# Folding the query squares of the grouped-query heads to 64 rows, and taking their roots in two parts

## The chip, the cores and the metric

The kernel runs on one core of a Trainium2 chip. The metric is the device time of one execution in microseconds (us); the time before is the median of three runs, 1474.04 us (1473.47 to 1475.6). The profile is one execution recorded by the hardware, with five compute queues: PE (TensorE matmuls; PEld is its weight loads), DVE (VectorE), ACT (ScalarE), POOL (GpSimd) and SP (which issues transfers). 0.2% of the time is 2.95 us.

## The reference, cut to what matters

One step of a two-layer backbone over 512 latent tokens and 128 prompt tokens (640 columns in all). The second layer's mixer is grouped-query attention: 8 query heads of width 128, 2 key/value heads. Queries and keys are normalised per token and head, then rotated, then used in a softmax:

```python
def rms_norm(x, g):
    y = xf * lax.rsqrt(jnp.mean(xf * xf, axis=-1, keepdims=True) + RMS_EPS)
    return (y * g.astype(jnp.float32)).astype(x.dtype)
...
    q = rms_norm(q.reshape(b, L, GQA_HEADS, GQA_HEAD_DIM), q_norm)
    q = apply_rope(q, cos, sin)
    o = attend_blocked(q, jnp.concatenate([k, c_k], axis=1), jnp.concatenate([v, c_v], axis=1), GQA_SCALE)
```

What the change touches is the reciprocal root of the mean square of each token's query, for one head: 640 numbers per head. The rotation does not alter the sum of squares, and the root is one factor per token, so the kernel applies it late, as a scale inside the softmax's exponential.

## The kernel before, in words

Activations lie with features on the 128 partitions and tokens on the columns. Every large product is made of three matmuls of split operands (a high and a low part, so that precision is near fp32): `mm3` at line 183 and `proj` at line 188.

The part that matters is the loop over the 8 heads at line 1906. In head h's turn the PE queue interleaves four kinds of work, each cut into pieces:

- `s0` to `s4`: scores of head h for token tiles 0 to 4 (tile 4 is the prompt), into a two-bank PSUM tile `gs` of which there are two. After a piece come a maximum (DVE, line 1858), a bias `gb` = maximum times root (DVE, line 1868), the exponential with the root as scale (ACT, line 1869), a reciprocal (DVE) and a scaling (POOL, line 393). For tile 0 the part from the bias on is a piece of its own, `x0`.
- `q0` to `q7`: the projection of head h+1's queries, `q0` to `q3` for columns 0 to 319 and `q4` to `q7` for columns 320 to 639. At the end of each half `done` (line 1827) copies the sum out of PSUM (`gqc`, ACT), squares it (`gsq`, ACT, line 1830), rotates it (`gqr`, four DVE operations), and splits the result into `gqh` (ACT) and `gql` (DVE), the score weights of the next turn.
- `t0` to `t4`, `v0` to `v4`, `pt` and `pv`: transposes and value products of head h-1. A transpose piece puts four 128x128 blocks into a PSUM bank `gt`, which `pt_split` (line 395) empties by an ACT copy (`gts_..h`) and a DVE subtraction (`gts_..l`). `pt` does the same for the prompt (`gtp`). All `v` pieces sum into one bank, `go`.
- `r`: the root of head h. Five matmuls have the squares of one token tile as weights and two columns of ones as the moving operand; each is recorded as two passes. Then ACT takes the logarithm and an exponential (lines 1841 and 1842).

The order of these pieces on PE is written out by hand in `GQA_ORDER` (line 1905), and `run` (line 115) ties each piece behind the matmul before it. The other engines' orders are made by a planner, which takes what is ready in the plan's own time, earlier program lines first. Buffers are given out by that planner too: a tile takes a buffer of its tag once all readers of the earlier tile there are done.

PSUM has eight banks. Four belong to the two `gs` tiles. The other four have the tag "m" (line 91) and serve every other PSUM tile of this loop: `gq` (one half of a projection), `gt`, `gtp`, `go`, `gop` and `gr` (the roots).

The weights of the next projection are also split within the turn: an ACT copy (line 173) and a DVE subtraction `wgq` (line 174) of 128x1024.

The planner's order and the buffers follow from these lines:

```python
            return psp.tile([P, 512], F32, tag="m", bufs=4, name=name)
...
        return tp.tile([P, T], F32, tag="t", bufs=3, name=name)
```

Of the kernel before, what the change touches and what calls it, by code (L numbers as in the profile page):

```python
# [11 lines left out]
F32 = mybir.dt.float32  # L12
F32R = mybir.dt.float32r
AF = mybir.ActivationFunctionType
ALU = mybir.AluOpType
# [3 lines left out]
P = 128  # L19
# [32 lines left out]
def body(ctx, tc, xT, vecs, crow, wm0, wm0g1, wm0g, wm1, wA, wNV, wNA, wMK, wMV, wOA, wGQ, wGK, wGV, wOC,  # L52
# [3 lines left out]
    V, S, G = nc.vector, nc.scalar, nc.gpsimd  # L56
# [32 lines left out]
    def bank(name, kind="m"):  # L89
        if kind == "m":  # L90
            return psp.tile([P, 512], F32, tag="m", bufs=4, name=name)
        return ypool["pool"].tile([P, 512], F32, tag=kind, bufs=ypool["tags"][kind], name=name)
# [10 lines left out]
    def tmp(name):  # L103
        return tp.tile([P, T], F32, tag="t", bufs=3, name=name)

    def f(ap):
        return ap.bitcast(F32)
# [7 lines left out]
    def run(pieces):  # L115

        for piece in pieces:
            with tc.issue_after(PE.last.ins):
                piece()
# [7 lines left out]
    def named(prefix, pieces):  # L127
        return {f"{prefix}{i}": piece for i, piece in enumerate(pieces)}
# [6 lines left out]
    ones = main.tile([P, P], F32, name="ones")  # L135
    V.memset(ones, 1.0)
    eps = main.tile([P, 1], F32, name="eps")
    V.memset(eps, EPS)
    lnsc = main.tile([P, 1], F32, name="lnsc")
# [9 lines left out]
    def vcol(i):  # L149
        return vec[:, i:i + 1]  # L150
# [17 lines left out]
    def unit(src, n, name, lo="v", pool=None, bufs=3):  # L168

        raw = load(src, n, name + "r")  # L170
        t = (pool or wp).tile([P, 2, 1024], F32R, tag="w", bufs=bufs, name=name)
        hi, lw = t[:, 0, :n], t[:, 1, :n]
        S.activation(hi, raw, AF.Copy)
        (V if lo == "v" else G).tensor_tensor(lw, raw, f(hi), ALU.subtract)
        return hi, lw

    def after(inst, fn):
        if inst is None:
            return fn()
        with tc.issue_after(inst.ins):  # L180
            return fn()
# [13 lines left out]
    class Norm:  # L195
# [19 lines left out]
        def rstd(self, i):  # L215
            c0, c1 = HALF[i]
            pss = bank(f"{self.name}p{i}")
            PE.matmul(pss[:, :HT], ones, self.acc[:, c0:c1], start=True, stop=i not in self.alone)
            if i in self.alone:
                PE.matmul(pss[:, :HT], ones, self.alone[i], start=False, stop=True)  # L220
            S.activation(self.rs[:, c0:c1], pss[:, :HT], AF.Ln, bias=eps, scale=1.0 / self.n)
            S.activation(self.rs[:, c0:c1], self.rs[:, c0:c1], AF.Exp, scale=-0.5)
            return self.rs
# [273 lines left out]
    def lazy(fn):  # L497
        box = []

        def get():  # L500
            if not box:
                box.append(fn())
            return box[0]
        return get
# [128 lines left out]
    for kk in range(4):  # L633
# [3 lines left out]
        for j in range(2):  # L637
            k = 2 * kk + j
            a, b = wh[:, 512 * j:512 * (j + 1)], wl[:, 512 * j:512 * (j + 1)]
            for i in range(5):  # L640
                c0, c1 = P * i, P * i + P
# [264 lines left out]
    for h in range(8):  # L906
        p, r = divmod(h, 2)
# [8 lines left out]
        qh, ql, ks = [t[r] for t in nqk[p]]  # L916
        pieces = named("s", sc)
# [60 lines left out]
    def mla_scores(h, pts, beside):  # L978
        r = h % 2
        ll = tiny.tile([P, 4], F32, tag="ll", bufs=4, name=f"ml{h}")  # L980

        def piece(j):
            qh, ql = mqs[h]
            pss = bank2(f"ms{h}_{j}")
            kh, kl = [t[0] for t in k_tiles(r, h // 2)]
            scores(pss, (qh[:, P * j:P * j + P], ql[:, P * j:P * j + P]), kh, kl)
            if j in beside:
                beside[j](pss[:, :, HT:HT + P])
            nm = tiny.tile([P, 1], F32, tag="nm", name=f"mn{h}_{j}")
            V.tensor_reduce(nm, pss[:, :, :HT], AX.XY, ALU.max, negate=True)  # L990
            pt = cp.tile([P, T], F32, tag="mp", bufs=8, name=f"mp{h}_{j}")
            exps[h, j] = S.activation(halves(pt), pss[:, :, :HT], AF.Exp, bias=nm, accum_out=ll[:, j:j + 1])
            softmax_tail(pt, ll[:, j:j + 1], f"mr{h}_{j}", T)
            pts.append(pt)
        return [lambda j=j: piece(j) for j in range(4)]
# [40 lines left out]
    for h in range(8):  # L1036
        p, r = divmod(h, 2)
# [5 lines left out]
        qh, ql = mqs[h]  # L1043
        beside = {1: tail.pop("pt"), 3: tail.pop("pv")} if h and r == 0 else {}
        pieces = named("s", mla_scores(h, pts, beside))
# [676 lines left out]
    gp = sb.enter_context(tc.tile_pool(name="gp", bufs=1, reuse_waits="tile"))  # L1722
# [91 lines left out]
    nc.gpsimd.dma_start(o_gv, gvf[:, :256])  # L1814

    gqs, gexp = {}, {}

    def gqa_q(h):
        get = lazy(lambda: after(gqs[h - 1][3][0] if h > 1 else None, lambda: unit(wGQ[h], 1024, f"wgq{h}", lo="v" if h == 1 else "v")))
        qh = gp.tile([P, T], F32R, tag="gqh", bufs=2, name=f"gqh{h}")  # L1820
        ql = gp.tile([P, T], F32R, tag="gql", bufs=2, name=f"gql{h}")
        rq = tiny.tile([P, 5], F32, tag="rq", bufs=2, name=f"rq{h}")
        sq = tmp(f"gsq{h}")
        gqs[h] = qh, ql, rq, []
        out = []
        for c, (c0, c1) in enumerate(HALF):
            def done(ps, c=c, c0=c0, c1=c1):
                qc = tp.tile([P, HT], F32, tag="u", bufs=7, name=f"gqc{h}{c}")
                gqs[h][3].append(S.activation(qc, ps[:, :HT], AF.Copy))
                S.activation(sq[:, c0:c1], qc, AF.Square)  # L1830
                qr = tp.tile([P, HT], F32, tag="u", bufs=7, name=f"gqr{h}{c}")
                rope(qr, qc, vcol(V_GQ), c, f"gqr{h}{c}")
                S.activation(qh[:, c0:c1], qr, AF.Copy)
                V.tensor_tensor(ql[:, c0:c1], qr, f(qh[:, c0:c1]), ALU.subtract)
            out += pieces_of(f"gq{h}{c}", qbank, get, hh, hl, list(range(KT)), c0, c1, done)

        def rstd():
            pr = bank(f"gr{h}")
            for j in range(5):
                PE.matmul(pr[:, 2 * j:2 * j + 2], sq[:, P * j:P * j + P], ones[:, 0:2], start=True, stop=True)  # L1840
            S.activation(rq, pr[:, 0:10].rearrange("p (a b) -> p a b", b=2)[:, :, 0], AF.Ln, bias=eps, scale=1.0 / P)
            S.activation(rq, rq, AF.Exp, bias=lnsc, scale=-0.5)
        return out + [rstd]

    def gqa_scores(h, pts):
        v = h // 4
        ll = tiny.tile([P, 5], F32, tag="lg", bufs=4, name=f"gl{h}")

        def piece(j):
            qh, ql, rq, _ = gqs[h]  # L1850
            q = qh[:, P * j:P * j + P], ql[:, P * j:P * j + P]
            nm = tiny.tile([P, 1], F32, tag="nm", name=f"gn{h}_{j}")
            nb = tiny.tile([P, 1], F32, tag="nb", name=f"gb{h}_{j}")
            pss = bank2(f"gs{h}_{j}")
            if j < 4:
                pt = gp.tile([P, T], F32, tag="gp", bufs=8, name=f"gp{h}_{j}")
                scores(pss, q, kTh[v], kTl[v])
                V.tensor_reduce(nm, pss[:, :, :HT], AX.XY, ALU.max, negate=True)
                src, dst, n = pss[:, :, :HT], halves(pt), T
            else:  # L1860
                pt = gp.tile([P, P], F32, tag="gpp", bufs=1, name=f"gp{h}_{j}")
                src = pss[:, 0, :P]
                mm3(src, *q, kTh[v][:, 640:768], kTl[v][:, 640:768], True, True)
                V.tensor_reduce(nm, src, AX.X, ALU.max, negate=True)
                dst, n = pt, P

            def weigh():
                V.tensor_tensor(nb, nm, rq[:, j:j + 1], ALU.mult)  # L1868
                gexp[h, j] = S.activation(dst, src, AF.Exp, bias=nb, scale=rq[:, j:j + 1], accum_out=ll[:, j:j + 1])  # L1869
                softmax_tail(pt, ll[:, j:j + 1], f"gr{h}_{j}", n)  # L1870
                pts.append(pt)
            return weigh

        box = []
        rest = {f"s{j}": (lambda j=j: piece(j)()) for j in range(1, 5)}
        return {"s0": lambda: box.append(piece(0)), "x0": lambda: box[0](), **rest}
# [22 lines left out]
        return {"pt": prompt_t, "pv": prompt, **t}  # L1899

    open_y(s=2)
    *qp, rstd = gqa_q(0)
    run(qp)
    tail, oG = {}, []
    GQA_ORDER = "s0 r x0 t0 q0 s1 t1 q1 t2 s2 q2 v0 t3 s3 q3 v1 t4 s4 pt q4 v2 q5 q6 v3 q7 v4 pv"
    for h in range(8):
        oG.append(gp.tile([P, T], F32, tag="go", bufs=8, name=f"oG{h}"))
        pts = []
        pieces = gqa_scores(h, pts)
        pieces["r"] = rstd  # L1910
        if h < 7:
            *qp, rstd = gqa_q(h + 1)
            pieces.update(named("q", qp))
        sequence(GQA_ORDER, {**pieces, **tail})
        tail = gqa_values(h, pts, oG[h])
# [181 lines left out]
```

## Time and profile before

| | us |
|---|---|
| median of three runs | 1474.04 |
| profiled execution | 1473.37 |
| its span | 1471.5 |
| one head's turn with all four kinds of work | 18.07 |
| PE busy in the span | 1439.2 (98%) |

The span runs from the first to the last recorded instruction; 1.87 us of the execution's own time lie around it. In a timeline a row gives start, duration, engine, line, operation, tiles written and read, and in brackets the idle time ahead of it with what ended it. Matmuls overlap, so that on PE the distance between two starts is the price of an instruction, and the duration is not.

### The profile page before, as it was taken

To read this page: it belongs to the slowest core of one execution; us is meant where nothing else is said; L and a number is where in the kernel's file an instruction comes from. 1 tells how busy PE (TensorE), PEld (TensorE's weight loads), DVE (VectorE), ACT (ScalarE), POOL (GpSimd) and SP (SyncE) were. 2 spreads that over 40 slices of the span, in tenths; PEclk is the share of its full clock that TensorE was granted. 3 is DMA by queue.
4 is the path that set the end of the run, shared out by engine and by line. 5 is a ranking of instruction groups with operands and counts; after the bars stand their busy time and mean duration, and the time that the engine had idled before them with its cause. 6 is when DMAs were issued, how large, how long until landed. Compare 5 with 4: busy or idle time off the path is not lost.

```text
span 1471.5 us, 25831 instructions
## 1 busy us (share of the span) xinstructions
PE 1439.2 (98%) x9764; PEld 1388.8 (94%) x9764; DVE 1235.1 (84%) x2391; ACT 783.9 (53%) x1539; POOL 173.9 (12%) x270
## 2 busy tenths in 40 slices
PE   5999999999999999999999999999999999999997
PEld 3989978889999999999999999989999999999997
DVE  5877798877998888965997888888899898989976
ACT  5446687763755555531223656672656555555443
POOL 0046645420000000000000122220000000000000
PEclk9999999999999999999999999999999999999999
DMA  9653431025165555569764310115245555548572
GB/s 372 212 161 125 145 115 44 15 89 184 48 213 165 169 168 170 181 233 321 235 223 150 97 33 30 45 44 185 87 167 187 179 177 182 177 143 296 184 270 72
DMA packets 79636, 231.48 MB, mean 157 GB/s; under 512 B 8856, under 2 KB 13240, under 8 KB 79128
## 3 DMA queue, kind: packets, MB, share of 16 engines
q1 hardware_dynamic: 77152, 225.43, 45.7%
q10 hardware_dynamic: 1944, 3.48, 0.7%
q8 instruction: 76, 1.25, 0.3%
q0 software_dynamic: 416, 0.93, 0.2%
q14 instruction: 48, 0.39, 0.1%
HBM read 193.15 MB, written 36.66 MB: 156 GB/s over the span
## 4 chain that ended last, share of the span: by engine, by line
PE 86%; DVE 6%; ACT 4%; issue 2%; DMA 2%; POOL 1%; DVEq 0%; ACTq 0%; POOLq 0%
PE fg L64 21%; PE fd L64 9%; PE fgo L64 5%; PE fo L64 5%; PE fu L64 4%; PE gq L64 3%; PE fdo L64 2%; PE gs L64 2%; PE go L64 2%; PE fuo L64 1%; PE nq L64 1%; PE gt L68 1%; PE nk L64 1%; PE gvp L64 1%; PE mod L64 1%
## 5 line engine op out<-in xcount | busy, mean ns | idle before, releaser
L1664 DVE SCALAR_TENSOR_TENSOR junk<-wm,cb 128x1024 bf16<-128x1024 f32 x88 | 107.2, 1218 | 6.4 <-DMA wm<-in_wm 5.5
L64 PE MATMUL gq<-h10h,wgq 128*128 128x320 f32 x256 | 65.8, 316 | 0.0
L267 POOL TENSOR_SCALAR h10h<-h10t,gs,mods 128x320 fp32r<-128x320 f32 x4 | 3.9, 990 | 429.4 <-DVE h10t L261 427.1
L1404 ACT ACTIVATE wY<-s 128x1024 fp32r<-128x1024 f32 x38 | 40.3, 1061 | 25.4 <-PE fg L64 21.4
L1932 POOL TENSOR_TENSOR xr<-xw,fn1rs 128x320 f32<-128x320 f32 x2 | 1.7, 862 | 412.8 <-ACT fn1rs L235 412.8
L1404 ACT ACTIVATE wZ<-s 128x1024 fp32r<-128x1024 f32 x38 | 40.1, 1056 | 16.0 <-PE fd L64 11.7
L1405 DVE TENSOR_TENSOR wZ<-s,wZ 128x1024 fp32r<-128x1024 f32 x38 | 46.3, 1219 | 1.6
L1405 DVE TENSOR_TENSOR wY<-s,wY 128x1024 fp32r<-128x1024 f32 x38 | 46.3, 1219 | 0.3
L64 PEld LDWEIGHTS gq<-h10h,wgq 128*128 128x128 f32 x256 | 44.9, 189 | 0.6
L1513 DVE TENSOR_TENSOR sg<-up,sg 128x640 f32<-128x640 f32 x38 | 31.2, 822 | 15.8 <-ACT sg L1512 15.0
L1512 ACT ACTIVATE sg<-fg 128x320 f32<-128x320 f32 x38 | 16.7, 438 | 48.4 <-PE fg L64 48.4
L1534 ACT ACTIVATE p<-fd 128x320 f32<-128x320 f32 x38 | 16.6, 438 | 44.1 <-PE fd L64 44.1
L64 PE MATMUL gq<-h10l,wgq 128*128 128x320 f32 x128 | 39.4, 308 | 0.0
L1869 ACT ACTIVATE gp<-gs,gb,rq 128x640 f32<-128x640 f32 (+1 forms) x40 | 31.8, 796 | 13.2 <-DVE gb L1868 11.8
L64 PE MATMUL fg<-h01E,wW 128*128 128x320 f32 x228 | 36.6, 309 | 0.5 <-DVE g L1544 0.5
L64 PE MATMUL fg<-h11N,wZ 128*128 128x320 f32 x228 | 36.7, 309 | 0.0
L64 PE MATMUL fg<-h01q,wX 128*128 128x320 f32 x228 | 36.7, 309 | 0.0
L64 PE MATMUL fu<-h11q,wX 128*128 128x320 f32 x228 | 36.6, 309 | 0.0
L64 PE MATMUL fd<-h11q,wZ 128*128 128x320 f32 x228 | 36.6, 309 | 0.0
L64 PE MATMUL fd<-h01q,wZ 128*128 128x320 f32 x228 | 36.5, 309 | 0.0
L64 PE MATMUL fg<-h01C,wY 128*128 128x320 f32 x228 | 36.5, 309 | 0.0
L64 PE MATMUL fg<-h11q,wX 128*128 128x320 f32 x228 | 36.5, 309 | 0.0
(3421 smaller groups left out, 5299.4 us busy)
## 6 DMA issues: line engine op xcount, KB each, us to landing
wm<-in_wm SPq DMA_DIRECT2D x48, 512.0 KB, 4.2
mraw<-in_wm SPq DMA_DIRECT2D x8, 1024.0 KB, 13.1
mraw<-in_wm SPq DMA_DIRECT2D x14, 512.0 KB, 4.1
wmv<-in_wm0g SPq DMA_DIRECT2D x8, 512.0 KB, 4.1
wm<-in_wm0g SPq DMA_DIRECT2D x8, 512.0 KB, 5.1
ruo<-in_wFO SPq DMA_DIRECT2D x8, 512.0 KB, 3.9
rgo<-in_wFO SPq DMA_DIRECT2D x8, 512.0 KB, 5.3
x<-in_xT SPq DMA_DIRECT2D x8, 320.0 KB, 5.4
```

The source lines that it names most:

```text
L64: cls.last = nc.tensor.matmul(*a, **k)
L68: cls.last = nc.tensor.transpose(*a, **k)
L267: G.tensor_scalar(h[:, c0:c1], t, self.gsl[:, k, 0:1], self.ml[:, self.sh + k, 0:1], ALU.mult, ALU.add)
L1404: S.activation(h, src, AF.Copy)
L1405: V.tensor_tensor(w_, src, f(h), ALU.subtract)
L1512: last = S.activation(sg[:, 0:HT], g[:, :HT], AF.Silu, scale=-1.0)
L1513: V.tensor_tensor(sg, up, sg, ALU.mult)
L1534: S.activation(p5, b5[:, :HT], AF.Copy)
L1664: V.scalar_tensor_tensor(junk, raw, 1.0, cb[:, c, :], ALU.mult, ALU.mult, accum_out=mods[l][:, j0 + i, c:c + 1])
L1869: gexp[h, j] = S.activation(dst, src, AF.Exp, bias=nb, scale=rq[:, j:j + 1], accum_out=ll[:, j:j + 1])
L1932: G.tensor_tensor(x[k][:, c0:c1], root[1][k], nrm.rs[:, c0:c1], ALU.mult)
```

## The change

The squares of a half are written in two pieces of 64 rows (features 0 to 63 and 64 to 127), both on partitions 0 to 63. A new tile `fold` receives their sums, so that 64 rows hold what 128 held: rows 0 to 63 of a column block carry one token tile and rows 64 to 127 the next. Block 0 holds tiles 0 and 1, block 1 tiles 2 and 3, and block 2 tile 4 on its first 64 rows. A constant `two` of two columns, with ones on the upper or the lower 64 rows, then gives both tiles' sums in one product. So there are three products per head in place of five.

The roots are taken in two parts: block 0 (`n`, or `early` for head 0) in the turn before, between `q6` and `v3`; blocks 1 and 2 (`r`) in the head's own turn, now between `s1` and `t1`. Each part has its own PSUM bank and its own logarithm and exponential. The bias `gb` moves from DVE to ACT, and `x0` directly follows `s0`. The `t` tag has three buffers as before, and each head now takes two of them. For the second half the folding stands ahead of the low part's subtraction.

```diff
+    two = gp.tile([P, 2], F32, name="two")
+    V.memset(two, 0.0)
+    for r in range(2):
+        V.memset(two[64 * r:64 * r + 64, r:r + 1], 1.0)
...
-        sq = tmp(f"gsq{h}")
+        sq = [tmp(f"gsq{h}{r}")[0:64] for r in range(2)]
+        fold = gp.tile([P, 3, P], F32, tag="gfold", bufs=2, name=f"gfold{h}")
+        a, b = [t.rearrange("p (j n) -> p j n", n=P) for t in sq]
...
+        def folded(i, r, j, n):
+            V.tensor_tensor(fold[64 * r:64 * r + 64, i:i + n, :], a[:, j:j + 2 * n - 1:2, :], b[:, j:j + 2 * n - 1:2, :], ALU.add)
...
-                S.activation(sq[:, c0:c1], qc, AF.Square)
+                for r in range(2):
+                    S.activation(sq[r][:, c0:c1], qc[64 * r:64 * r + 64], AF.Square)
...
-                V.tensor_tensor(ql[:, c0:c1], qr, f(qh[:, c0:c1]), ALU.subtract)
+                if c == 0:
+                    V.tensor_tensor(ql[:, c0:c1], qr, f(qh[:, c0:c1]), ALU.subtract)
+                    folded(0, 0, 0, 1)
+                    folded(0, 1, 1, 1)
+                else:
+                    folded(1, 0, 2, 2)
+                    folded(1, 1, 3, 1)
+                    V.tensor_tensor(ql[:, c0:c1], qr, f(qh[:, c0:c1]), ALU.subtract)
...
-        def rstd():
-            pr = bank(f"gr{h}")
-            for j in range(5):
-                PE.matmul(pr[:, 2 * j:2 * j + 2], sq[:, P * j:P * j + P], ones[:, 0:2], start=True, stop=True)
-            S.activation(rq, pr[:, 0:10].rearrange("p (a b) -> p a b", b=2)[:, :, 0], AF.Ln, bias=eps, scale=1.0 / P)
-            S.activation(rq, rq, AF.Exp, bias=lnsc, scale=-0.5)
-        return out + [rstd]
+        def rstd(at):
+            pr = bank(f"gr{h}{at}")
+            for i in ((0,), (1, 2))[at]:
+                rows = slice(0, P if i < 2 else 64)
+                PE.matmul(pr[:, 2 * (i - at):2 * (i - at) + 2], fold[rows, i, :], two[rows], start=True, stop=True)
+            t = rq[:, (0, 2)[at]:(2, 5)[at]]
+            S.activation(t, pr[:, 0:2 + at], AF.Ln, bias=eps, scale=1.0 / P)
+            S.activation(t, t, AF.Exp, bias=lnsc, scale=-0.5)
+        return out + [lambda: rstd(0), lambda: rstd(1)]
...
-                V.tensor_tensor(nb, nm, rq[:, j:j + 1], ALU.mult)
+                S.activation(nb, nm, AF.Copy, scale=rq[:, j:j + 1])
...
-    *qp, rstd = gqa_q(0)
-    run(qp)
+    *qp, early, rstd = gqa_q(0)
+    run(qp + [early])
...
-    GQA_ORDER = "s0 r x0 t0 q0 s1 t1 q1 t2 s2 q2 v0 t3 s3 q3 v1 t4 s4 pt q4 v2 q5 q6 v3 q7 v4 pv"
+    GQA_ORDER = "s0 x0 t0 q0 s1 r t1 q1 t2 s2 q2 v0 t3 s3 q3 v1 t4 s4 pt q4 v2 q5 q6 n v3 q7 v4 pv"
...
-            *qp, rstd = gqa_q(h + 1)
+            *qp, pieces["n"], rstd = gqa_q(h + 1)
```

## The prediction

> **What bounds the kernel now.** I read the page first: its span, its engines and the chain that ended last.
>
> ```profile
> span 1471.5 us, 25831 instructions
> ...
> PE 1439.2 (98%) x9764; PEld 1388.8 (94%) x9764; DVE 1235.1 (84%) x2391; ACT 783.9 (53%) x1539; POOL 173.9 (12%) x270
> ...
> PE 86%; DVE 6%; ACT 4%; issue 2%; DMA 2%; POOL 1%; DVEq 0%; ACTq 0%; POOLq 0%
> ```
>
> PE is the bound. Next come the busy times of one full turn (head 2's scores, head 3's projection, head 1's values), in the order span, PE, PEld, DVE, ACT, POOL, and PE's waits in the whole loop, 841 to 993 us.
>
> ```profile
> 881.21:899.28 18.07, 18.07 (x127) 17.29 (x125) 14.54 (x33) 11.39 (x27) 3.74 (x5) 1.00 0.10 30
> ```
>
> ```profile
> PE gs L64 <- ACT gp L1869: 0.4, 2, 0.2
> PE gop L64 <- DVE gtp6l L402: 0.3, 1, 0.3
> PE gs L64 <- ACT gqh L1833: 0.3, 1, 0.3
> PE gs L64 <- DVE gql L1834: 0.2, 1, 0.2
> PE gop L64 <- ACT gtp6h L401: 0.2, 1, 0.2
> ```
>
> In a full turn PE is busy all 18.07 us, at the full clock (1.00). In the loop's 152 us it waits 1.4 us. So a PE pass taken out of heads 1 to 6 is gained in full as long as nothing else makes PE wait, and no gain beyond the passes and those 1.4 us exists. DVE has 3.5 us to spare per turn, ACT 6.7.
>
> **The passes.** The rows of the root's tiles, and PE's timeline around it:
>
> ```profile
> L64 PE MATMUL gr<-ones,gsq x80: 166/251/251, 849.6 to 972.5; 128*128 128x2 f32 x80
> ```
>
> ```profile
> 866.39 0.60 PE L68 MATMUL gt<-ident,gp 128*128 128x128 f32 x4
> 866.75 0.40 PE L64 MATMUL gq<-h10h,wgq 128*128 128x320 f32 x1
> ...
> 877.73 0.39 PE L64 MATMUL go<-gts_3h,gvh 128*128 128x512 f32 x1
> 877.96 0.40 PE L64 MATMUL go<-gts_3h,gvl 128*128 128x512 f32 x1
> ...
> 881.21 1.17 PE L64 MATMUL gr<-ones,gsq 128*128 128x2 f32 x10
> 882.25 0.64 PE L68 MATMUL gt<-ident,gp 128*128 128x128 f32 x4
> 882.64 0.39 PE L64 MATMUL gq<-h10h,wgq 128*128 128x320 f32 x1
> ```
>
> ```profile
> 980.30 0.47 PE L64 MATMUL go<-gts_2h,gvh 128*128 128x512 f32 x1
> 980.61 0.39 PE L64 MATMUL go<-gts_2h,gvl 128*128 128x512 f32 x1
> ```
>
> 80 passes are 8 heads of 5 products of 2 passes. One head's ten occupy PE from 881.21 to 882.25, 1.04 us, so 0.104 each. The transposes that follow take 0.39 to the next start, against 0.36 behind scores (866.39 to 866.75); `r` moves from ahead of `t0` to ahead of `t1`, so that 0.03 moves with it. The first value matmul behind a group of prompt transposes takes 0.31 (980.30 to 980.61) against 0.23 in the middle (877.73 to 877.96): each new group of root passes between other work costs 0.08 behind it.
>
> After: `r` has 4 passes, 0.42; `n` has 2, 0.21, and the 0.08 behind it. Heads 1 to 6: -1.04 + 0.42 + 0.29 = -0.33 each, -2.0. Head 0 also has `early` (0.29): -0.04. Head 7 has no `n`: -0.62. Sum -2.66. Passes over 64 rows are not in this trace: between 0.052 (half) and 0.104, and I take 0.104, since the row nearest is the full pass; the low end would give another -0.8 (two passes, eight heads).
>
> [...]
>
> **ACT and DVE.** Prices of what is added and taken away:
>
> ```profile
> L1830 ACT ACTIVATE gsq<-gqc x16: 459/471/473, 845.8 to 970.3; 128x320 f32<-128x320 f32 x16
> ```
>
> ```profile
> L1868 DVE TENSOR_TENSOR gb<-gn,rq x40: 141/152/369, 852.1 to 981.6; 128x1 f32<-128x1 f32 x40
> ...
> L1841 ACT ACTIVATE rq<-gr,eps x8: 266/267/268, 850.8 to 972.8; 128x5 f32<-128x5 f32 x8
> L1842 ACT ACTIVATE rq<-rq,lnsc x8: 287/289/302, 851.1 to 973.3; 128x5 f32<-128x5 f32 x8
> ```
>
> ACT per head: two more squares, 2 x 0.47 (64 rows by 320 columns; nearest row 128x320; not below 0.47/2 if rows counted); one more logarithm and exponential, 0.27 + 0.29; five biases, each between nothing and the 0.27 of the 128x5 logarithm, which I take: 1.35. Together +2.85, so 14.2 of 18.07, and hidden under PE if nobody waits for one of them. DVE per head: -5 x 0.15 = -0.76; four foldings, three of 64x128 at 0.27 (the 128x128 subtraction `gtp0l` below) and one of 64x256 at 0.42 (the row below): +1.23. Together +0.47, so 15.0 of 18.07. The three memsets are paid once, at about 0.15 each (the 128x1 row), and lie in DVE's idle 0.68 ahead of 845.85, which the row of `gqr` there shows.
>
> ```profile
> 843.21 0.42 DVE L1795 TENSOR_TENSOR gvl<-gvp,gvh 128x256 fp32r<-128x256 f32 x1
> ...
> 845.85 0.55 DVE L1733 SCALAR_TENSOR_TENSOR gqr<-gqc,vec,tg 128x320 f32<-128x320 f32 x1 [0.68 <-ACT gqc L1829]
> ```
>
> [...]
>
> **The wait that the change adds.** `n` needs an "m" bank ahead of `v3`. Here is who holds the four in the turn of head 1 (PE, then ACT and DVE):
>
> ```profile
> 869.91 0.39 PE L64 MATMUL go<-gts_0h,gvh 128*128 128x512 f32 x1
> ...
> 873.51 0.60 PE L68 MATMUL gt<-ident,gp 128*128 128x128 f32 x4
> ...
> 874.24 0.30 PE L68 MATMUL gtp<-ident,gp 128*128 128x128 f32 x1
> 874.29 0.40 PE L64 MATMUL gq<-h10h,wgq 128*128 128x320 f32 x1
> ```
>
> ```profile
> 875.52 0.59 ACT L401 ACTIVATE gts_4h<-gt 128x512 fp32r<-128x512 f32 x1
> 876.03 1.75 DVE L174 TENSOR_TENSOR wgq<-wgq3r,wgq 128x1024 fp32r<-128x1024 f32 x1
> ...
> 877.71 0.48 DVE L1834 TENSOR_TENSOR gql<-gqr,gqh 128x320 fp32r<-128x320 f32 x1
> ```
>
> ```profile
> 948.24 1.75 DVE L174 TENSOR_TENSOR wgq<-wgq7r,wgq 128x1024 fp32r<-128x1024 f32 x1
> ```
>
> ```profile
> 878.11 0.68 DVE L402 TENSOR_TENSOR gts_4l<-gt,gts_4h 128x512 fp32r<-128x512 f32 x1
> ...
> 878.78 0.27 DVE L402 TENSOR_TENSOR gtp0l<-gtp,gtp0h 128x128 fp32r<-128x128 f32 x1
> ```
>
> At `n`'s place, 877.73, `go` is held until `v4`, `gq` until `q7`, `gt` of `t4` until 878.79 (878.11 + 0.68) and `gtp` until 879.05. All four are taken, and `n` would stand 878.79 - 877.73 = 1.06 us. PE takes its matmuls in order, so `v3`, `q7`, `v4` and the next `s0` queue behind it, and a PE without slack never gets it back. The head of the delay is the 128x1024 subtraction at 876.03. PE's place and this chain both move 0.6 earlier with the shorter `r`, so the gap stays. On DVE, two biases leave ahead of the subtraction (-0.3), which may run in less than 1.75; the two foldings of the first half (0.54 at most, earlier in program order than the split) can come ahead of the split. On ACT, a second square and a bias come ahead of `gts_4h` (875.52), about 0.7, but DVE stays in the subtraction until 877.78 anyway. I take 0.8 per turn, between 0 (the split planned ahead of the subtraction: 875.52 + 0.59 + 0.7 + 0.68 = 877.5) and 1.6 (1.06 + 0.54). It holds in heads 1 to 5, whose five turns have the big subtraction (876.03 to 948.24): head 0's turn has no `t` or `go`, and in head 6's no weights are left to split. 5 x 0.8 = +4.0.
>
> **The rest.** `r` now follows `s1`. In the before, `t1` follows it at 884.48; without the ten passes that is 883.4. The second half's squares and rotation:
>
> ```profile
> 879.97 0.47 ACT L1830 ACTIVATE gsq<-gqc 128x320 f32<-128x320 f32 x1
> ```
>
> ```profile
> 881.68 0.49 DVE L1736 TENSOR_TENSOR gqr<-gqr,gqr21b 128x320 f32<-128x320 f32 x1
> 882.09 0.82 DVE L1858 TENSOR_REDUCE gn<-gs 128x1 f32<-128x640 f32 x1
> ...
> 884.48 0.60 PE L68 MATMUL gt<-ident,gp 128*128 128x128 f32 x4
> ```
>
> Both squares end by 880.9 (879.97 + 2 x 0.47). Foldings put between 881.68 and the maximum end near 882.8, 0.6 ahead of 883.4: no wait. Put behind the maximum they end at 883.6, a wait of 0.2. I take nothing. Head 0 has no tail to cover its chain: the second half's low part (DVE) feeds `s2` there, the folding (0.69) stands ahead of it, and PE comes sooner. I take +0.3 (0 to 0.7). In head 7 ACT's extra work lies ahead of the waits for `gp` and `gtp6h`; half of its -0.62 is lost, +0.3. `x0` starts sooner, but it was awaited twice at 0.2 only: nothing.
>
> Sum: -2.66 + 4.0 + 0.6 = +1.9 on the profiled execution's 1473.37, so 1475.3. That execution lies 0.67 under the median of 1474.04; by the median 1476.0.
>
> **Rivals.** *No bank wait*: the planner puts the split ahead of the big subtraction, or that one elsewhere. For it: DVE has 3.5 us free per turn. Against: the big one was put in that place five times (876.03 to 948.24). -2.66 + 0.6 = -2.1, 1471.9; at best, with the 0.8 of cheaper passes and the 1.4 of old waits, -4.9 and 1469.1. *Long bank wait* (slower): both foldings and all of ACT's extra stand ahead of the split, 1.6 per turn: 8.0 - 2.1 = +5.9, 1479.9. It decides from 1.0 per turn, where the sum passes +2.95. *`r` waits for the folding*: with the biases ACT runs the squares behind `oG` and the exponential, and PE stands 0.5 in seven turns on top: +5.4, 1479.5. *The change does not fold*: excluded, the products are written out in the code, and 48 records must be left of 80.
>
> **How the numbers follow.** Chances: forecast 0.42, no bank wait 0.33, long wait 0.15, `r` 0.10. 0.2% is 2.95 us, about what a measurement of this kernel can tell from no change: below 1471.1 lies most of the better half of the first rival, 0.21; above 1477.0 lie the last two and a fifth of the forecast, 0.33; between them 0.46. The likeliest case's own range is 0.4 to 1.3 per turn, 1474.0 to 1478.5. With the others cut at a tenth each side: 1470.3 to 1480.3.
>
> **What would show it.** Right: 48 `gr` records; a turn of PE with a wait ahead of `gr` of `n` of about 0.8 us in heads 1 to 5, put down to `gts_4l` or `gtp`; turns of some 18.5 us. Wrong: turns of 17.74 without a wait (no bank wait); a wait at the second `gr` put down to the folding; an `n` that starts before its bank's readers have ended would make the bank argument void.

## The result, and the profile after

The changed kernel takes 1483.16 us (median of six runs, 1482.22 to 1486.17) against 1474.95 for the kernel before beside it: a ratio of 1.0058 (95% interval 1.0048 to 1.0068; below, such an interval stands in square brackets), slower by 8.2 us. The forecast was 1476.0, with a range of 1470.3 to 1480.3. The profiled execution of the change took 1486.17, the longest of its runs, and that of before 1473.37, just under the shortest of its own (1473.47). Their spans therefore differ by 12.9, and the parts below account for that. About 3.0 + 1.6 of it is the distance of the two executions from their medians.

The page of the changed kernel:

```profile
span 1484.4 us, 25849 instructions
...
PE 1441.7 (97%) x9732; PEld 1388.6 (94%) x9732; DVE 1238.6 (83%) x2386; ACT 803.3 (54%) x1611; POOL 173.1 (12%) x270
```

PE has 32 records fewer and is busy longer; ACT has 72 more. The next views cut the loop at the first matmul of each head's `s0`, and show heads 0, 1, 4 and 6. Columns are the span, then busy time with instructions of PE, PEld, DVE, ACT and POOL, then the granted TensorE clock, the DMA share and GB/s. Before:

```profile
848.64:861.62 12.98, 12.57 (x87) 11.96 (x86) 10.37 (x25) 7.89 (x18) 3.54 (x4) 1.00 0.01 2
861.62:880.29 18.67, 18.42 (x125) 17.36 (x125) 15.45 (x36) 12.00 (x29) 4.33 (x6) 1.00 0.17 47
916.42:934.49 18.07, 18.07 (x127) 17.28 (x126) 14.54 (x33) 11.39 (x28) 3.74 (x5) 1.00 0.10 32
952.55:970.62 18.07, 18.07 (x127) 17.29 (x126) 16.16 (x36) 13.54 (x31) 4.82 (x6) 1.00 0.20 66
```

After, the same turns:

```profile
851.26:867.86 16.60, 14.16 (x83) 13.34 (x83) 11.83 (x25) 10.99 (x30) 3.46 (x4) 0.90 0.00 1
867.86:887.19 19.33, 18.38 (x122) 16.97 (x121) 15.61 (x35) 14.45 (x37) 4.43 (x6) 1.00 0.11 32
925.00:943.90 18.90, 18.04 (x122) 16.98 (x122) 14.94 (x32) 13.97 (x37) 3.87 (x5) 1.00 0.09 29
962.81:982.00 19.19, 18.38 (x122) 17.00 (x122) 16.89 (x35) 15.63 (x40) 5.31 (x5) 1.00 0.17 55
```

The stage behind head 7 has no cut of its own, so I take the first `fgo`, well after the loop (the first start of this row; before, then after):

```profile
L64 PE MATMUL fgo<-op9a,wXo x12: 307/308/309, 1323.6 to 1352.0; 128*128 128x320 f32 x12
```

```profile
L64 PE MATMUL fgo<-op9a,wXo x12: 307/308/309, 1336.4 to 1364.9; 128*128 128x320 f32 x12
```

From head 7's `s0` (970.62 before, 982.00 after) to it are 353.0 and 354.4 us.

| part | before | after | difference |
|---|---|---|---|
| head 0 | 12.98 | 16.60 | +3.6 |
| head 1 | 18.67 | 19.33 | +0.7 |
| heads 2 to 5, each | 18.07 | 18.90 | +0.83, together +3.3 |
| head 6 | 18.07 | 19.19 | +1.1 |
| head 7 and the stage behind it | 353.0 | 354.4 | +1.4 |

That is 10.1. Another 2.6 lies ahead of head 0's `s0` (848.64 against 851.26), and the last 0.1 behind the first `fgo`. All but 0.2 of the 2.6 is there before the first changed PE instruction, with PE's work the same. Over all kernels here this start varied from 848.6 to 852.1, so I count it as scatter between executions.

PE's waits in the changed loop (engine, what waits, what ended the wait; total us, times, longest):

```profile
PE gr L64 <- DVE gts_4l L402: 3.5, 4, 0.9
PE gr L64 <- DVE gfold L1833: 2.9, 5, 1.2
PE gs L64 <- ACT gp L1888: 2.1, 4, 0.8
PE oc3a L64 <- DVE ocw L174: 0.5, 1, 0.5
PE go L64 <- ACT gts_0h L401: 0.4, 1, 0.4
PE oc6a L64 <- DVE ocw L174: 0.3, 1, 0.3
```

The first row is the forecast's wait for a bank. The next two, 5.0 us in nine waits, are what it did not have: PE waits for the folding itself, and at `s2` for an exponential. The timeline of PE places them; in brackets stands the idle time ahead of the row and what ended it:

```profile
854.60 0.69 PE L64 MATMUL gr<-two,gfold 128*128 128x2 f32 x4 [0.45 <-DVE gfold L1833]
...
857.17 0.56 PE L64 MATMUL gs<-gkh,gqh 128*128 128x320 f32 x2 [0.80 <-ACT gp L1888]
...
866.66 0.38 PE L64 MATMUL gr<-two,gfold 128*128 128x2 f32 x2 [1.19 <-DVE gfold L1833]
...
941.01 0.38 PE L64 MATMUL gr<-two,gfold 128*128 128x2 f32 x2 [0.86 <-DVE gts_4l L402]
```

The first three are all of head 0. Heads 2 to 5 have only the wait at `n`, 0.86 to 0.88 each. Heads 1, 6 and 7 have the pair at `r` and `s2` again (0.39 and 0.56, 0.49 and 0.31, 0.39 and 0.42).

### The profile page after: what moved, and what is told of

Its sections match the earlier page's. It is cut to its first block, busy times and chain, and to the rows that moved or that the text cites. A ratio compares the mean times of both kernels' runs of the same rounds, so it can differ in the third digit from the quotient of the medians.

```text
span 1484.4 us, 25849 instructions
## 1 busy us (share of the span) xinstructions
PE 1441.7 (97%) x9732; PEld 1388.6 (94%) x9732; DVE 1238.6 (83%) x2386; ACT 803.3 (54%) x1611; POOL 173.1 (12%) x270
## 3 DMA queue, kind: packets, MB, share of 16 engines
q8 instruction: 76, 1.25, 0.3%
## 5 line engine op out<-in xcount | busy, mean ns | idle before, releaser
L64 PE MATMUL fg<-h01N,wZ 128*128 128x320 f32 x228 | 36.6, 309 | 0.0
```

Source lines behind the costliest of these rows:

```text
L64: cls.last = nc.tensor.matmul(*a, **k)
```

## The experiments

Each kernel differs from the changed one, or from the one before, by the edit shown. Times are medians of several runs. The runs came in three groups (experiments 1 to 4, 5 to 8, 9 to 11), each on one chip with the kernel before timed beside it (1474.55, 1475.42, 1474.40), and the ratio is to that. Every profile is one execution.

**1. `n` put last in the turn.** Does the wait at `n` come from its place among the bank holders?

```diff
-... q5 q6 n v3 q7 v4 pv"
+... q5 q6 v3 q7 v4 pv n"
```

> The changed kernel with the first two tiles' root (n) moved from between q6 and v3 to behind pv; nothing else. Theory A (PE stands at n: for an m bank until gts_4l is subtracted, 1.0 us in each of heads 2 to 5, and in head 0 for the folding, 1.35 us): these 5.4 us go, turns of heads 2 to 5 fall from 18.91 to 17.9, and the time falls from 1483.2 to about 1478. Theory B (ACT's extra work, the bias and the squares, sets the pace wherever n stands): turns stay above 18.6 and the time above 1482.

Measured: 1479.72 us, 1.0034 [1.0022, 1.0045]. The bank wait ahead of `n` is gone from heads 2 to 5. From head 2's to head 3's `s0`:

```profile
883.77 0.54 PE L64 MATMUL gs<-gkh,gqh 128*128 128x320 f32 x2
...
901.53 0.54 PE L64 MATMUL gs<-gkh,gqh 128*128 128x320 f32 x2
```

That is 17.76, or 0.31 under the turn of before, close to the passes' gain of the prediction (0.33), once nothing waits. The next three turns took 17.96 to 18.20, and in head 6 a projection waits 0.94 for the bank of the previous head's sum instead. Some 5 of the 8.2 us remain, which is more than the 3.5 that Theory A left, and they lie in heads 0, 1, 6 and 7.

**2. The bias back on DVE.** Is the bias's move to ACT what makes `r` and `s2` late?

```diff
-                S.activation(nb, nm, AF.Copy, scale=rq[:, j:j + 1])
+                V.tensor_tensor(nb, nm, rq[:, j:j + 1], ALU.mult)
```

> The changed kernel with the bias gb back on DVE; n stays ahead of v3. Theory A: the wait at n in heads 2 to 5 stays between 0.8 and 1.1 us; only head 0 gains, where s2 waited 0.8 us for an exponential and the TensorE clock then stood at half for 3.5 us: about -2, 1481. Theory B: the waits go with ACT's 1.4 us per turn, turns near 18.1, time near 1477.

Measured: 1490.31 us, 1.0103 [1.0088, 1.0119], another 7 us slower than the change. The theory missed. PE, and then DVE ahead of the same place, in head 2's turn:

```profile
902.16 0.35 PE L64 MATMUL gr<-two,gfold 128*128 128x2 f32 x2 [1.69 <-DVE gr_4r L392]
```

```profile
898.63 1.76 DVE L174 TENSOR_TENSOR wgq<-wgq4r,wgq 128x1024 fp32r<-128x1024 f32 x1
...
900.72 0.57 DVE L1833 TENSOR_TENSOR gfold<-gsq,gsq 64x128 f32<-64x128 f32 x2
901.32 0.69 DVE L402 TENSOR_TENSOR gts_4l<-gt,gts_4h 128x512 fp32r<-128x512 f32 x1
```

The big subtraction and both foldings stand ahead of the split that frees the bank, and with five 0.15 us operations moved `gql` does too. The wait doubles to 1.64 to 1.69. This is the size that the prediction's rival of the long bank wait gave (1.6), but not its cause, since the biases that were to burden ACT are not there. In head 4 the TensorE clock also fell to half behind that wait (0.57 from 941.90 to 945.40), and the turn took 21.22 against 19.65 to 19.68 for heads 2, 3 and 5. In heads 2 to 5 of the change the big subtraction and the foldings stand ahead of the split as well, but the subtraction starts some 0.7 earlier, as seen from `n`, and takes 1.23:

```profile
937.62 1.23 DVE L174 TENSOR_TENSOR wgq<-wgq6r,wgq 128x1024 fp32r<-128x1024 f32 x1
...
939.23 1.00 DVE L1833 TENSOR_TENSOR gfold<-gsq,gsq 64x128 f32<-64x128 f32 x2
940.26 0.69 DVE L402 TENSOR_TENSOR gts_4l<-gt,gts_4h 128x512 fp32r<-128x512 f32 x1
```

**3. The kernel before with only its bias on ACT.**

```diff
-                V.tensor_tensor(nb, nm, rq[:, j:j + 1], ALU.mult)
+                S.activation(nb, nm, AF.Copy, scale=rq[:, j:j + 1])
```

> The kernel before with the bias gb on ACT, nothing else changed. Theory A: full turns stay at 18.07 us since PE waits for nothing there; head 0 and head 7, which wait for exponentials, lose up to 1 us together: 1475 to 1476. Theory B: turns above 18.3, time above 1478.

Measured: 1476.48 us, 1.0014 [1.0004, 1.0023], 1.9 us slower. Full turns stay at 18.06 to 18.07. In the profile the loss is not in heads 0 and 7, as expected, but behind the loop: 354.2 from head 7's `s0` (972.21) to the first `fgo`, against 353.0. The two `oc` waits of the change's table come back there, at the same 0.5 and 0.3.

In experiment 2, the change with the bias on DVE, both `oc` waits are gone and this stretch takes 353.3 (984.74 to 1338.0) against the change's 354.4. So most of the +1.4 in the last row of the table goes with the bias on ACT.

**4. `n` into a bank of its own.** The product was written into the second bank of the prompt's score tile, which no longer needs it.

```diff
-            pr = bank(f"gr{h}{at}")
+            pr = bank(f"gr{h}{at}") if at or not h else spare[h]
...
+                spare[h + 1] = pss[:, 1, :]
```

> The changed kernel with n at its place ahead of v3, but its product written into the second, unused bank of the prompt tile's score tile gs, so that it needs no m bank. Theory A with the bank alone: the waits at n in heads 2 to 5 go fully, turns 17.9. Theory A with the folding next in line: the second folding of the first half ends 0.7 us ahead of the bank's release, so that the wait falls from 1.02 to about 0.3, turns near 18.2, time near 1480. Theory B: turns stay at 18.9.

Measured: 1493.24 us, 1.0127 [1.0112, 1.0142]. The wait did not go away but changed its owner:

```profile
906.52 0.38 PE L64 MATMUL gs<-two,gfold 128*128 128x2 f32 x2 [2.44 <-ACT gp L1889]
```

The dependence is kept by tile, so `n` now waited for every reader of the scores, the exponential among them. The run therefore says nothing of banks against foldings; experiment 9 does.

**5. Both: `n` last and the bias on DVE.**

> The changed kernel with the first two tiles' root behind pv and the bias gb back on DVE. Theory (three separate costs: the bank at n, ACT's bias, the folding's place on DVE): against the first experiment the waits for ACT go (s2 of heads 0, 1 and 6, q0 behind oG, 0.5 us in the stage after the loop), about -2.5, so 1477; turns of heads 2 to 5 at 17.76. Rival (the bias has no price of its own, the rest is the folding): 1479 to 1480.

Measured: 1479.03 us, 1.0025 [1.0015, 1.0035], 2 more than expected and in the rival's range. The full turns came out at 17.86 to 17.90. The two largest kinds of wait left:

```profile
PE gr L64 <- DVE gfold L1833: 2.5, 5, 1.0
PE gs L64 <- ACT gp L1888: 1.8, 5, 0.6
```

So neither the bank nor the bias makes `r` late. The longest of them, in head 6, is behind a weight split of the next stage on DVE (`ocw`, 1.23 us from 958.83). In head 0 the clock fell to half here too, as at the end of this document; the 15.43 that head 0 takes holds some 1.5 of that.

```profile
961.23 0.67 PE L64 MATMUL gr<-two,gfold 128*128 128x2 f32 x4 [0.97 <-DVE gfold L1833]
```

**6. The same with `r` later.**

```diff
-... s0 x0 t0 q0 s1 r t1 q1 t2 s2 ...
+... s0 x0 t0 q0 s1 t1 q1 r t2 s2 ...
```

> As the last one (n behind pv, bias on DVE), with the second root r moved from ahead of t1 to ahead of t2. Theory: the waits of r for the folding in heads 0, 6 and 7 (0.45 to 0.5 us each, with 0.16 of refill) go, about -1.5 to -2: 1475 to 1475.5. Rival (r's wait only hides a later one, s2's wait for the first exponential): 1477.

Measured: 1478.44 us, 1.0019 [1.0005, 1.0032]. Heads 2 to 5 fall to 17.76 to 17.77 each, but in heads 0 and 7 `r`'s wait becomes one of 1.55 and 1.05 ahead of `s2`, and in head 6 one of 0.73 ahead of `t2`. The rival had it right: what comes late is the folding, and a later root passes that on to the exponential.

**7. The foldings issued in the root's pieces**, on the kernel of experiment 6: they come later in the program, so that DVE's other work goes first.

```diff
-                    folded(0, 0, 0, 1)
-                    folded(0, 1, 1, 1)
...
-                    folded(1, 0, 2, 2)
-                    folded(1, 1, 3, 1)
...
+            if at == 0:
+                folded(0, 0, 0, 1)
+                folded(0, 1, 1, 1)
+            else:
+                folded(1, 0, 2, 2)
+                folded(1, 1, 3, 1)
```

> As e6 (n behind pv, r ahead of t2, bias on DVE), with the foldings issued in the root's own pieces, so that the planner ranks them behind the maximum and the split. Theory: turns of 17.75, the maximum of tile 0 no longer stands behind the foldings, so that head 0 takes about 13.2: time 1473 to 1474.5, level with or under the kernel before. Rival: the foldings come too late and r waits for them: 1476 or more.

Measured: 1486.77 us, 1.0070 [1.0055, 1.0085]. Heads 2 to 5 stay at 17.76 to 17.77, and the others pay more:

```profile
PE gr L64 <- DVE gfold L1833: 7.4, 4, 3.0
PE gr L64 <- ACT gp L1890: 2.6, 1, 2.6
```

The theory missed and the rival had it right. `r` waits 1.67, 2.33 and 2.97 in heads 0, 1 and 7 (the fourth wait of the first row, 0.41, is that of `n` in head 0), and 2.55 in head 6, which the trace puts down to an exponential. The same foldings cost nothing in four heads and these waits in the other four, by where they stand on DVE.

**8. The root in two parts without folding.** The kernel before with `n` (4 passes) last and `r` (6 passes) ahead of `t1`, one square per half, the bias on DVE.

```diff
+        def rstd(at):
+            pr = bank(f"gr{h}{at}")
+            j0, j1 = ((0, 2), (2, 5))[at]
+            for j in range(j0, j1):
+                PE.matmul(pr[:, 2 * (j - j0):2 * (j - j0) + 2], sq[:, P * j:P * j + P], ones[:, 0:2], start=True, stop=True)
...
-    GQA_ORDER = "s0 r x0 t0 q0 s1 t1 q1 ...
+    GQA_ORDER = "s0 x0 t0 q0 s1 r t1 q1 ... q5 q6 v3 q7 v4 pv n"
```

> The kernel before with the roots in two parts (n behind pv with 4 passes, r ahead of t1 with 6), without folding: one square per half, bias on DVE. Theory: no waits for a folding and none for a bank, one more group of passes at 0.08 to 0.1: turns 18.15 to 18.2, time 1475 to 1476. Rival (splitting the root is itself what costs): turns above 18.4, time above 1477.

Measured: 1474.01 us, 0.9991 [0.9981, 1.0000], level with before and 1 under the theory. `r` never waits; the waits left are these:

```profile
PE gs L64 <- ACT gp L1871: 0.9, 1, 0.9
PE go L64 <- ACT gts_0h L401: 0.4, 1, 0.4
PE gs L64 <- DVE gql L1834: 0.3, 1, 0.3
```

The first is ahead of `s2` in head 0. It is there although nothing is folded, so it belongs to the root's split and new place; head 0 takes 13.33, against 12.98 before.

Against experiment 5, which differs by the folding, with its squares and passes, alone, head by head: head 0 13.33 against 15.43, head 1 18.63 against 19.58, heads 2 to 5 18.08 against 17.88, head 6 18.07 against 19.84, and from head 7's `s0` to the `fgo` 351.6 against 353.5. The folding gains 0.2 in four heads. It costs 1 to 2 in heads 1, 6 and 7 (with the stage behind), and in head 0 some 0.6 besides the 1.5 of the clock.

**9. The same with `n` ahead of `v3`.** The bank wait by itself, in a kernel without any folding.

```diff
-... q5 q6 v3 q7 v4 pv n"
+... q5 q6 n v3 q7 v4 pv"
```

> The split kernel without folding (bias on DVE) with n ahead of v3, as the changed kernel has it. Theory of the bank: n stands until gts_4l is subtracted, with no folding and no second square about: 0.9 to 1.1 us in each of heads 1 to 5, turns 19.1 to 19.3, time 1479.5 to 1481. Rival (the wait at n came from the foldings ahead of the split): turns 18.1 to 18.3, time 1474.5 to 1475.

Measured: 1480.97 us, 1.0045 [1.0029, 1.0060]. Five waits, as expected:

```profile
PE gr L64 <- DVE gr_4r L392: 5.1, 5, 1.1
```

```profile
902.36 0.51 PE L64 MATMUL gs<-gkh,gqh 128*128 128x320 f32 x2
...
918.72 0.58 PE L64 MATMUL gr<-ones,gsq 128*128 128x2 f32 x4 [1.12 <-DVE gr_4r L392]
...
921.80 0.51 PE L64 MATMUL gs<-gkh,gqh 128*128 128x320 f32 x2
```

A turn grows from 18.08 to 19.44 where the wait is 1.12 (902.36 to 921.80), and to 19.30 in heads 2, 4 and 5, where it is 0.98. So a wait shown as 0.98 costs 1.22, and one of 1.12 costs 1.36. The bank wait needs no folding. The trace names `gr_4r`, a reciprocal that stands on DVE right behind the split, as what ended it; that the split is the true owner rests on the change's own rows and on the prediction's list of holders.

**10. Two squares, no folding.** Experiment 8 with each square as two 64-row operations on ACT.

```diff
-                S.activation(sq[:, c0:c1], qc, AF.Square)
+                for r in range(2):
+                    S.activation(sq[64 * r:64 * r + 64, c0:c1], qc[64 * r:64 * r + 64], AF.Square)
```

> The split kernel without folding (n behind pv, bias on DVE), with each half's square made in two ACT operations of 64 rows, as folding needs them. It has ACT's part of the folding (0.94 us per head) without DVE's. Theory (DVE's foldings delay the rotation, the maximum and the low part): head 0 at 13.3 to 13.8, no waits for a root, 1474 to 1475. Rival (ACT's second square is what heads 0, 1, 6 and 7 lose): head 0 near 15, 1477 to 1478.

Measured: 1473.96 us, 0.9993 [0.9982, 1.0004]. ACT's second square costs nothing that can be measured; only head 6 is 0.4 longer (18.49). What hurts in heads 0, 1, 6 and 7 is thus, by elimination, the additions on DVE and their place ahead of the low part; the squares also lie on other partitions here than in a kernel that folds, which no run tells apart.

**11. Folding only where it pays.** Experiment 8 with the folding in heads 2 to 5, and `r` ahead of `t2` in the turns of heads 3 to 5.

```diff
+    FOLDED = (2, 3, 4, 5)
...
-        sequence(GQA_ORDER, {**pieces, **tail})
+        order = GQA_ORDER.replace("r t1 q1 t2", "t1 q1 r t2") if h in (3, 4, 5) else GQA_ORDER
+        sequence(order, {**pieces, **tail})
```

> The split kernel (n behind pv, bias on DVE) with folding for heads 2 to 5 alone, where the turns have slack on DVE and ACT; heads 0, 1, 6 and 7 keep one square per half and five products. In turns 3 to 5 r stands ahead of t2. Theory (folding pays 0.2 to 0.3 us in a full turn and costs only where no spare work covers it): turns 3 to 5 at 17.8 rather than 18.08, head 0 at 13.3, turn 6 without a wait: 0.5 to 1 us under the split kernel, 1473 to 1474. Rival (folding costs wherever it stands): 1476.

Measured: 1472.66 us over eleven runs, 0.9994 [0.9985, 1.0004]: not told apart from before. Heads 2 to 5 came to 17.90, 17.77, 17.76 and 17.99, each against 18.08 in experiment 8, and head 1, whose turn holds the `n` of head 2, to 18.37 against 18.63. All that folding gains here is thus some 1.2 us, less than a measurement of this kernel can tell.

## Why the prediction was wrong, step by step

**The bound: right. The passes: right in number and sum, each term a little off.** There are 48 records of the root's matmuls, and a turn without a wait takes 17.76 (with `n` last) where 17.74 was worked out. That is in part luck. Head 4's `r`, two full passes and two of 64 rows, takes 0.51 to the next start where the sum had 0.42, and `n` behind `pv` takes 0.20 (901.33 to 901.53 in experiment 1) where it had 0.29 with what stands behind it:

```profile
928.14 0.59 PE L64 MATMUL gr<-two,gfold 128*128 128x2 f32 x4
928.65 0.66 PE L68 MATMUL gt<-ident,gp 128*128 128x128 f32 x4
```

The more in `r` lies with the 64-row passes. Where the trace of the change keeps them apart, in head 1, the two take 0.31 to the next start; six full passes ahead of the same work, in experiment 8, take 0.58, some 0.1 each:

```profile
871.80 0.38 PE L64 MATMUL gr<-two,gfold 64*128 64x2 f32 x2
872.11 0.66 PE L68 MATMUL gt<-ident,gp 128*128 128x128 f32 x4
```

```profile
885.40 0.73 PE L64 MATMUL gr<-ones,gsq 128*128 128x2 f32 x6
885.98 0.63 PE L68 MATMUL gt<-ident,gp 128*128 128x128 f32 x4
```

The sum took a pass over 64 rows to be as dear as a full one; it was dearer by some 0.05, and why is not shown. The weight load itself was not what made it dearer: the 16 loads of 64 rows took 184 ns on average, the 32 of 128 rows 188, and all 48 between 182 and 190.

**The wait for a bank: right in mechanism and size, wrong in what it costs and in which heads.** 0.86 to 0.88 was shown against 0.8 forecast, put down to `gts_4l` as written. It is the bank and not the folding: in head 4 PE came to `n` at 940.15 (941.01 - 0.86), the folding was done at 940.23 and the split at 940.95. `v3`, whose operands had been there since 935.28 (the row of `gts_3l`, 934.59 and 0.69 long), started behind it at 941.25, so PE kept its order as the prediction had it. In the size two misses cancel: the subtraction took 1.23, not 1.75, and the two foldings ahead of the split 1.00, not 0.54 (rows at 937.62 and 939.23 above). The wait was there in heads 2 to 5, not in head 1. There PE had already lost 0.39 and 0.56 in the same turn, and the planner had put the split (883.50 to 884.19) ahead of the big subtraction (884.11), so that `n` found its bank free at 884.33. The wait costs more than its idle time: 18.90 - 17.76 = 1.14 for 0.87 here, 1.22 for 0.98 in experiment 9; in both, `n`'s place within the turn is a part of that. So four heads paid 4.6, where the sum had 5 x 0.8 = 4.0. The waits that were to make turns of "some 18.5" made 18.9.

**"The rest": this step failed.** It took `r`'s wait as nothing, head 0 at +0.3 (0 to 0.7), head 7 at +0.3 and the stage behind the loop at nothing.

- *Head 0* lost 3.6. The prediction saw that it has no tail to cover its chain and that the folding stands ahead of the rest of DVE's work, and still bounded it by the folding's own 0.7. Experiment 8, with the root in two parts and no folding, cuts the loss up. It takes 13.33 itself, 0.35 above before. The rest lies between the first matmuls of `s0`, `s2`, `s4` and the next `s0`. From `s0` to `s2` the change takes 5.91 against 5.35: `r` waits 0.45 for the folding, and the 0.80 at `s2` replaces the 0.93 of experiment 8; that is 0.32 of the 0.56, and the rest has no wait to its name. From `s2` to `s4` it takes 5.17 against 3.63, with no wait: here the TensorE clock fell to half (the 0.90 of the head's row), which is shown below. From `s4` on it takes 5.52 against 4.35: `n` waits 1.19 for the folding of head 1's first half. 0.35 + 0.56 + 1.54 + 1.17 = 3.6.
- *`r` waits nothing* held in heads 2 to 5 alone. The step placed the foldings in the rows of one full turn, head 1's to head 2's, and gave its answer to all. In heads 1, 6 and 7 DVE has other work at that place: in the windows it goes from 14.94 busy in head 4 to 15.61 and 16.89 in heads 1 and 6. In head 1 the second half's rotation starts behind the split of the next projection's weights (866.64 to 867.87). In head 6 a weight split of the next stage comes first, while the squares were done at 964.24:

```profile
964.20 1.23 DVE L174 TENSOR_TENSOR ocw<-ocw1r,ocw 128x1024 fp32r<-128x1024 f32 x1
...
965.74 0.71 DVE L1833 TENSOR_TENSOR gfold<-gsq,gsq 64x256 f32<-64x256 f32 x2
```

  The prediction's own sign of being wrong, a wait at the second `gr` put down to the folding, thus came in four heads. The rival of this name (chance 0.10) had the wait and about its size (0.5 per turn), but not the cause. It made ACT late with the squares, by the biases; with the bias back on DVE `r` still waits (experiment 5), and with the squares doubled but nothing folded it does not (experiment 10). It also had too many heads and no wait behind `r`.
- *The stage behind the loop* lost 1.4, some 1.1 of which comes with the bias on ACT (experiments 2 and 3). The prediction priced the bias well (0.27 against the 0.294 measured below), but put no wait down to it behind the loop.

```profile
L1887 ACT ACTIVATE gb<-gn,rq x40: 278/294/299, 855.8 to 993.1; 128x1 f32<-128x1 f32 x40
```

**What hid what.** "DVE has 3.5 us to spare per turn" was the average of a full turn and was treated as cover in all eight. Experiments 8 and 10 against 5 show that the 1.23 us of foldings per head, not ACT's squares, cost 1 to 2 us in each of heads 1, 6 and 7 and 0.6 in head 0, the clock aside. Four good heads could win 0.3 each at best.

**The sum.** By medians the change is +8.2; in the two profiled executions the parts above hold 10.1. There the bank wait with the passes makes +3.3 in heads 2 to 5 (4.6 - 1.2), head 0 adds 3.6, and heads 1, 6 and 7 with the stage behind add 3.2; of head 6's 1.1, some 0.3 stays without a name. Which parts are smaller in a median run the record does not show; the clock's 1.5 may not be in all of them. The range ended at 1480.3 because the rival for `r`, which already stood on top of the bank wait (1479.5), had only 0.5 per turn for everything that waits: no wait at `n` for its own folding, no half clock, nothing behind the loop.

## What to carry to other kernels

A wait for a shared buffer can be read in advance, from the last readers of its holders in the trace of before; its cost per turn is above the idle time shown (1.14 for 0.87 and 1.22 for 0.98 here). Work called hidden has to be placed in the turn with the least cover, the first, the last and those that share the engine with the next stage, since the average slack of a middle turn says nothing of them. Where a planner orders an engine, moving a few 0.15 us operations to or from it can move everything else on it (7 us by the medians of experiment 2, with a spell of half clock in its profile), so that such an edit needs its own price, apart from that of the operations.

## What the runs showed of the hardware

**The clock.** In head 0 of the change the granted clock fell to half for 3.5 us, behind the waits of 0.45 and 0.80 (same columns as the windows above):

```profile
856.00:858.00 2.00, 1.20 (x7) 0.93 (x6) 0.70 (x2) 1.93 (x5) 0.50 (x1) 0.91 0.00 0
857.60:861.10 3.50, 3.50 (x15) 3.50 (x15) 0.90 (x2) 1.98 (x5) 1.48 (x2) 0.51 0.00 0
```

3.5 us at half speed cost 1.5: from the first matmul of `s2` to that of `s4` the change takes 5.17 (857.17 to 862.34). In experiment 1, with the same two waits (0.45 and 0.80), the same work takes 3.62 (855.74 to 859.36), and the stretch ran at full speed with 30 matmul records in 4.00 us:

```profile
857.00:861.00 4.00, 4.00 (x30) 4.00 (x29) 2.66 (x6) 2.71 (x7) 1.61 (x2) 1.00 0.00 0
```

The drop was there in head 0 of the profiled executions of experiments 4, 5, 6 and 7, in head 1 of experiment 4 and in head 4 of experiment 2, but nowhere in the loop of experiment 1, so the waits alone do not decide it. The kernel before and experiments 3 and 8 to 11 had none either, among them experiment 9 with five bank waits of about 1 us. What brings the drop on is not shown, and it stays open whether it is what spreads the runs of the change over 4 us.

**DVE beside POOL.** A folding of 64x128 takes 0.276 at least, 0.286 in the median over both shapes, and 0.718 at most, with two together in 1.00 (the row at 939.23 above) instead of 0.57 (the one at 900.72):

```profile
L1833 DVE TENSOR_TENSOR gfold<-gsq,gsq x32: 276/286/718, 850.0 to 984.4; 64x128 f32<-64x128 f32 x24, 64x256 f32<-64x256 f32 x8
```

In head 0 such a pair (865.61 to 866.61) lies beside the scaling of `gp` on POOL:

```profile
865.39 1.08 POOL L393 TENSOR_SCALAR gp<-gp,gr_3r 128x640 f32<-128x640 f32 x1 [1.95 <-DVE gr_3r L392]
```

The prediction had 0.54 for the pair. Over the loops of all 13 profiled executions the two go together. None of the 23 pairs of 0.57 to 0.58 overlaps a scaling, and all 24 of 1.00 to 1.01 do, by 0.86 to 0.88. The 128x1024 subtraction `wgq` shows the same: all 45 of 1.75 to 1.76 overlap a scaling, by 0.67 to 0.69, and the rest take 1.21 to 1.23. So in the kernel before it was the subtraction that met the scaling, and in the change, where the subtraction comes earlier, it is the foldings. In ten other overlaps over their whole length, the subtractions of `wgq` and `ocw` kept their 1.21 to 1.25 and the row of the scaling was the long one (1.41 to 2.01). No run took POOL's scaling away, so that it is the cause was not tried.
